# Expert outputs of a routed trunk layer: 29 experts store their slots' products plainly, and each token's row gathers its four

## The chip, the cores and the metric

The kernel runs on one core of one Trainium2 chip. The metric is the device time of one execution in microseconds (us). Before the change, three runs gave 1467.29, 1469.84 and 1470.49 us; the median is 1469.84 us.

## The reference, cut to what matters

512 tokens of width 1024 go through one layer: a mixing sublayer with a LayerNorm, then a routed feed-forward sublayer with a LayerNorm. All data are float32. The change touches only how the outputs of the routed sublayer come together:

```python
top_val, top_idx = lax.top_k(logits, TOP_K)          # 4 of 32 experts for each token
gate = jax.nn.softmax(top_val, axis=-1)
...
gu = xb @ w_gu[e] + b_gu[e]                          # 1024 x 2048 weights for each expert
...
return act @ w_dn[e] + b_dn[e]                       # 1024 x 1024
...
y_sorted = out[dest] * gate.reshape(-1)[order][:, None]
y = jnp.zeros_like(xt).at[tok_sorted].add(y_sorted)  # each token: the sum of its four
...
h = layer_norm(DEEPNORM_ALPHA * h + ffn, ln2_g[l], ln2_b[l])
```

## The kernel before, in words

**Stages.** Up to about 390 us of the profiled span the kernel computes the mixing sublayer, the router and the slots. Each expert has up to 96 slots (`CAP`), a low part of 64 and a high part of 32; the high part is computed only where the expert has more than 64 tokens (`past64`, a branch on a loaded count; always for experts 0 and 31). In this execution 14 of the experts 0 to 30 ran their high part, 13 of them below expert 29; of experts 6 to 26 it is 10. Then `experts` (from line 1365) runs over the 32 experts, and from about 1434 us `tail` does the last LayerNorm and the output.

**Weights.** Each expert needs 12 chunks of 1 MB: eight row blocks of `w_gate_up` and four of `w_down`. All are loaded on SP's queue (line 1193) into a ring of SBUF slots, 18 at the start, whose order is the table `RING`. A load waits until PE has read what stood in its slot, and on the landing of an earlier load: the queue's instructions take their landing counters `DMAHW0` to `DMAHW7` in turn, all DMAs that SP and ACT issue share these eight, and a DMA is issued only when the one before it on its counter has landed. So at most eight are under way.

**Order of one expert.** With k from 0 to 7, `gu_low` multiplies the tokens of the expert by a chunk (line 1285), and `gu_high` those of slots 64 to 95 (line 1290). At k = 3, `load_gu(e + 1)`, `load_dn(e)` and the gather of the tokens of expert e + 2 (`expert_gather`, line 1217, POOL, an indirect DMA of 96 rows of 4 KB) are put in, and the transposes of expert e + 1. Then comes `swiglu`, and then `dn` of the expert before: PE runs gu(e), then dn(e - 1). The tile framework keeps each engine's instructions in the order in which the code gives them.

**Outputs.** `dn` multiplies by `w_down` into PSUM, low part as 128 partitions x 512 (two halves of the columns x 64 slots), high part as 128 x 256 (four quarters x 32 slots). Its inner `out` scales by the gate on ACT into the tile `eo` (line 1335), and an indirect DMA on POOL (line 1336) adds these 128 rows into the DRAM tensor `yd`, at the rows of their tokens. There are 45 such adds, 31 low (experts 0 to 30) and 14 high. `yd` is cleared by three DMAs of `routing_setup` (line 1162) at the start of the program, from a zero tile, on SP. Expert 31 is not added: its products stay on chip and PE sends them to the tokens by 0/1 matrices in `tail`.

**End.** `tail_rows` (line 1529) adds `yd` into the residual `res` by four DMAs of 512 KB on POOL that add to SBUF what they load. `tail` then adds expert 31 and normalizes.

One other place is used below, the loads of the down biases in `bias_loads`, on SP, into 96 partitions x 512 of which the source repeats 32 rows three times:

```python
nc.sync.dma_start(self.braw[q], bass.AP(tensor=b.tensor, offset=b.offset + 512 * q, ap=[[0, 3], [D, NE], [1, 512]]))   # L988
```

Of the kernel before, what the change touches and what calls it, by code (L numbers as in the profile page):

```python
# [24 lines left out]
F32 = mybir.dt.float32  # L25
F32R = mybir.dt.float32r
BF = mybir.dt.bfloat16
I32 = mybir.dt.int32
U32 = mybir.dt.uint32
AF = mybir.ActivationFunctionType  # L30
OP = mybir.AluOpType
# [6 lines left out]
KAPPA = math.exp(-0.5)  # L38
ALPHA = 2.0 ** 0.25
CAP = 96  # L40
OB = 104
PADROWS = 128

# [83 lines left out]
class Trunk:  # L127
# [4 lines left out]
    def setup(self):  # L132
        nc, tc, a = self.nc, self.tc, self.a
        self.cp = cp = self.ctx.enter_context(tc.tile_pool(name="const", bufs=1))
        self.dp = self.ctx.enter_context(tc.tile_pool(name="dram", bufs=1, space=DRAM))
        self.ident = cp.tile([128, 128], F32, name="ident")
        nc.gpsimd.dma_start(self.ident, a["consts"][:, 0:128])
        self.C = cp.tile([128, CONSTS.shape[1] - 128], F32, name="cst")
        self.c = {k: self.C[:, o - 128:o - 128 + n] for k, (o, n) in CAT.items() if k != "ident"}
        e = cp.tile([128, 2], F32, name="eps")  # L140
        self.eps = {v: e[:, q:q + 1] for q, v in enumerate((1e-5, 64e-5))}
        for v, col in self.eps.items():
            nc.vector.memset(col, v)
        self.wd = self.dp.tile([6, T], F32, name="wd")
        self.tab = self.dp.tile([NE * 512, 2], F32, name="tab")
        self.hd = self.dp.tile([T + PADROWS, D], F32, name="hd")
        self.yd, self.yo = (self.dp.tile([T + PADROWS, D], F32, name=n) for n in ("yd", "yo"))

    def params(self):
        nc, a, cp = self.nc, self.a, self.sp  # L150
# [952 lines left out]
    def route_slots(self):  # L1103
# [16 lines left out]
        nc.vector.tensor_tensor(V0, oh, wide(self.val, NE), OP.mult)  # L1120
        nc.vector.tensor_tensor(self.S, c["iota96"].unsqueeze(1).to_broadcast([128, 16, CAP]), wide(dest, CAP), OP.is_equal)

    def route_table(self):
        nc = self.nc
        V = self.V.rearrange("p i k e -> p (i k) e")
        p = self.tbank()
        for k in range(16):
            nc.tensor.matmul(p[0:CAP, 0:64], self.S[:, k], V[:, k], start=(k == 0), stop=(k == 15))
        nc.vector.tensor_scalar(self.tt[:, 0:32], p[0:CAP, 0:32], self.c["pad"][0:CAP], None, OP.add)
        nc.vector.tensor_copy(self.tt[:, 32:64], p[0:CAP, 32:64])  # L1130
# [19 lines left out]
    def routing_setup(self):  # L1150
        nc, sp, c = self.nc, self.sp, self.c
        self.onesb = self.cp.tile([128, 128], BF, name="onesb")
        nc.gpsimd.memset(self.onesb, 1.0)
        self.trib = self.cp.tile([128, 128], BF, name="trib")
        nc.vector.tensor_copy(self.trib, c["mask2"][:, 0:128])
        self.mkb = self.cp.tile([128, NT, NE], BF, name="mkb")
        self.sel0 = self.expert_sel(0)
        self.ro = self.cp.tile([128, 3, NT, 4], F32, name="ro")
        z = self.Sb[0].rearrange("p j v -> p (j v)")
        for c0, n in ((0, 384), (384, 384), (768, 256)):  # L1160
            nc.sync.dma_start(self.hd[T:T + PADROWS, c0:c0 + n], z[:, :n])
            nc.sync.dma_start(self.yd[:, c0:c0 + n].rearrange("(i p) c -> p i c", p=128), z[:, :n].unsqueeze(1).to_broadcast([128, NT + 1, n]))


# [151 lines left out]
    def dn(self, e, aT, wd, n):  # L1316
        nc, mm = self.nc, self.nc.tensor.matmul
        p0 = self.mps.tile([128, 512], F32, name="dn0")
        if e == 0:
            self.dn2 = self.mps.tile([128, 512], F32, name="dn2")[:, 0:256]  # L1320
        p2 = self.dn2

        def high():
            for k in range(NK):
                for c in range(4):
                    mm(p2[32 * c:32 * c + 32], aT[:, 4 + k % 2, 32 * (k // 2):32 * (k // 2) + 32], wd[k][:, 256 * c:256 * c + 256],  # L1326
                       start=(k == 0), stop=(k == NK - 1), skip_group_check=True)

        for k in range(NK):
            for h in range(2):  # L1330
                mm(p0[64 * h:64 * h + 64], aT[:, k % 4, 64 * (k // 4):64 * (k // 4) + 64], wd[k][:, 512 * h:512 * h + 512], start=(k == 0), stop=(k == NK - 1))  # L1331
        def out(g, p):
            w = 512 >> g
            o = self.mw.tile([128, w], F32, name=f"eo{g}")
            nc.scalar.activation(o, p, AF.Copy, scale=self.gate[:, g, e:e + 1])  # L1335
            return nc.gpsimd.indirect_dma_start(out=self.yd.rearrange("t (c f) -> (t c) f", f=w),  # L1336
                                                out_offset=bass.IndirectOffsetOnAxis(ap=self.sidx[:, g, e:e + 1], axis=0),
                                                in_=o, in_offset=None, compute_op=OP.add)

        if e < NE - 1:  # L1340
            first = out(0, p0)

        def past():
            high()
            if e < NE - 1:
                second = out(1, p2)
                self.tc.declare_no_dep(second.ins, first.ins, reason="rows of other slots")
                if self.added is not None:
                    self.after(second, self.added, mybir.DependencyClass.Sync)

        self.past64(n, past)
        if e < NE - 1:
            self.added = first
        if e == NE - 1:
            his = []
            for g, p in enumerate((p0, p2)):
                hi, lo = self.slast[2 * g:2 * g + 2]
                his.append(nc.scalar.activation(hi, p, AF.Copy, scale=self.gate[:, g, e:e + 1]))
                nc.vector.scalar_tensor_tensor(lo, p, self.gate[:, g, e:e + 1], hi, OP.mult, OP.subtract)
            self.warm = self.mw.tile([128, 1], F32, name="warm")  # L1360
            w = nc.scalar.activation(self.warm, self.eps[1e-5], AF.Sqrt)
            for h in his:
                self.after(w, h)

    def experts(self):
        self.xg = [self.mw.tile([128, D], F32, name=f"xg{q}") for q in range(2)]
        xs, xT = {}, {0: self.first_xT()}
        wg, pend, self.added = self.load_gu(0), None, None
        self.route_slots()
        for e in range(NE):  # L1370
            w = wg
            t, sel = xT.pop(e)
            n = self.fill(e)
            p = self.gu(t, sel)
            for k in range(NK):
                self.gu_low(p, k, t, w[k])
                if e == 0:
                    self.gu_high(p, k, t, w[k])
                elif k % 4 == 3:
                    self.past64(n, lambda: [self.gu_high(p, z, t, w[z]) for z in range(k - 3, k + 1)])  # L1380
                if e == 0:
                    if k == 0:
                        self.route_counts()
                        self.route_table()
                        self.tables()
                        xs[1] = self.expert_gather(1)
                    elif k < 5:
                        self.out_init(k - 1)
                if k == 3:
                    if e + 1 < NE:  # L1390
                        wg = self.load_gu(e + 1)
                    wd = self.load_dn(e)
                    if e + 2 < NE:
                        xs[e + 2] = self.expert_gather(e + 2)
                if k == (6 if e == 0 else 3) and e + 1 < NE:
                    xT[e + 1] = self.expert_xT(e + 1, xs.pop(e + 1))
            a = self.swiglu(p)
            if e == NE - 1:
                self.most = self.nc.values_load(self.mxi[0:1, 0:1], min_val=0, max_val=T)
                self.tail_setup()  # L1400
                aT = self.swiglu_T(a)
            if pend:
                self.dn(*pend)
            if e == NE - 1:
                self.tail_rows()
            pend = (e, aT if e == NE - 1 else self.swiglu_T(a), wd, n)
        self.dn(*pend)
# [99 lines left out]
    def tail_setup(self):  # L1507
# [14 lines left out]
        for q, p in enumerate(self.P):  # L1522
            g = q > 1
            m = c["par"][:, q:q + 1] if not g else c["quad"][:, q - 2:q - 1]
            nc.vector.tensor_scalar(p, iota, tk[:, g:g + 1], m, OP.is_equal, OP.mult)

    def tail_rows(self):
        for i in range(NT):
            self.nc.gpsimd.dma_start(self.res[i], self.yd[i * 128:i * 128 + 128], accum_op=OP.add)  # L1529

    def tail(self, out):
# [5 lines left out]
        for i in range(NT):  # L1537
            t = slice(128 * i, 128 * i + 128)
            ps.append([self.tbank() if n == "tr" else self.mps.tile([128, 512], F32, name=n) for n in (("gu0", "gu1"), ("gu2", "tr"), ("tr", "tr"), ("dn0", "dn2"))[i]])
            for q in range(2):  # L1540
# [5 lines left out]
                for x in range(2):  # L1546
                    for z in range(2):
                        mm(p[:, 256 * x:256 * x + 256], self.P[2 + 2 * q + x][:, t], self.slast[2 + z], start=False, stop=x == z == 1)  # L1548
        s = [self.chunk()[0] for _ in range(2)]
        xs = [s[i // 2][:, 1024 * (i % 2):1024 * (i % 2) + 1024] for i in range(NT)]  # L1550
        self.stores = [[] for _ in range(NT)]


# [137 lines left out]
```

## Time and profile before

| what | us |
|---|---|
| runs, lowest / median / highest | 1467.29 / 1469.84 / 1470.49 |
| the profiled execution | 1465.28 |
| its span in the trace | 1463.5 |
| PE busy (matmuls) | 1334.6 (91%) |
| DVE busy | 448.4 (31%) |
| ACT busy | 289.5 (20%) |
| POOL busy | 206.8 (14%) |
| bytes moved, mean rate | 461.88 MB, 316 GB/s |
| the 45 adds of line 1336, issue to landing, min/median/max | 5.8/9.5/11.3 |

The profiled execution is 4.56 us below the median of the runs; 1.8 us of it lie outside the span. Times in the rows below are in us from the start of the span. [...] A DMA share is the mean busy share of the core's 16 DMA engines in the stretch.

### The profile page before, as it was taken

To read this page: it belongs to the slowest core of one execution; us is meant where nothing else is said; L and a number is where in the kernel's file an instruction comes from. 1 tells how busy PE (TensorE), PEld (TensorE's weight loads), DVE (VectorE), ACT (ScalarE), POOL (GpSimd) and SP (SyncE) were. 2 spreads that over 40 slices of the span, in tenths; PEclk is the share of its full clock that TensorE was granted. 3 is DMA by queue.
4 is the path that set the end of the run, shared out by engine and by line. 5 is a ranking of instruction groups with operands and counts; after the bars stand their busy time and mean duration, and the time that the engine had idled before them with its cause. 6 is when DMAs were issued, how large, how long until landed. Compare 5 with 4: busy or idle time off the path is not lost. (4 is left out here: it accounts for less than half of the span.)

```text
span 1463.5 us, 19946 instructions
## 1 busy us (share of the span) xinstructions
PE 1334.6 (91%) x7860; PEld 623.9 (43%) x7861; DVE 448.4 (31%) x1070; ACT 289.5 (20%) x617; POOL 206.8 (14%) x190
## 2 busy tenths in 40 slices
PE   7899978998999999987899999999879878899995
PEld 5677878876533333322233333333323222333323
DVE  5767687788521112111111121111111111211114
ACT  4444342453011111110001111111100100111103
POOL 1211236241001100110001111011100100010100
PEclk9999996899999999999999999999999999999998
DMA  7222233346899999999999999999999999999974
GB/s 253 73 58 72 52 79 99 132 141 269 297 364 375 396 385 403 396 390 395 403 403 397 396 398 399 406 394 394 391 389 402 394 404 395 400 395 415 408 297 118
DMA packets 95232, 461.88 MB, mean 316 GB/s; under 512 B 18084, under 2 KB 26692, under 8 KB 45962
## 3 DMA queue, kind: packets, MB, share of 16 engines
q1 hardware_dynamic: 79962, 435.61, 75.9%
q0 software_dynamic: 10592, 20.49, 6.5%
q10 hardware_dynamic: 4560, 4.15, 0.9%
q8 instruction: 82, 1.34, 0.4%
q14 instruction: 36, 0.29, 0.1%
HBM read 445.97 MB, written 18.10 MB: 317 GB/s over the span
## 5 line engine op out<-in xcount | busy, mean ns | idle before, releaser
L1285 PE MATMUL gu<-wc,xT 128*64 128x512 f32 x2048 | 486.5, 603 | 65.1 <-DMA wc<-w_gate_up 62.2
L1285 PEld LDWEIGHTS gu<-wc,xT 128*64 128x64 f32 x2048 | 143.1, 137 | 388.5 <-issue 243.1
L1298 DVE TENSOR_SCALAR glu<-gu 128x256 f32<-128x256 f32 (+1 forms) x64 | 35.6, 556 | 829.1 <-PE gu L1290 376.6
L1331 PE MATMUL dn<-wc,aT 128*64 128x512 f32 x1024 | 247.5, 603 | 4.2 <-PEq L1278 2.4
L1299 ACT ACTIVATE glu<-glu 128x256 f32<-128x256 f32 (+1 forms) x64 | 33.5, 524 | 543.1 <-DVE glu L1298 543.1
L1217 POOL DMA_INDIRECT xg<-hd,gidx x31 | 30.9, 998 | 670.8 <-PE tr L1230 660.8
L1331 PEld LDWEIGHTS dn<-wc,aT 128*64 128x64 f32 x1024 | 65.1, 136 | 118.9 <-issue 102.3
L1290 PE MATMUL gu<-wc,xT 128*32 128x512 f32 x960 | 111.5, 596 | 0.0
L1336 POOL DMA_INDIRECT yd<-eo,sidx x45 | 70.1, 1557 | 275.2 <-ACT eo L1335 275.2
L222 PE MATMUL pi<-xhi,whi 128*128 128x512 f32 x152 | 65.0, 428 | 15.9 <-ACT whi L172 8.9
L1231 ACT ACTIVATE xT<-tr 128x384 f32<-128x384 f32 x62 | 29.8, 490 | 181.1 <-PE tr L1230 181.1
L223 PE MATMUL pi<-xlo,whi 128*128 128x512 f32 x152 | 63.7, 419 | 0.5 <-DVE xlo L173 0.5
L224 PE MATMUL pi<-xhi,wlo 128*128 128x512 f32 x152 | 62.8, 413 | 0.0
L1290 PEld LDWEIGHTS gu<-wc,xT 128*32 128x32 f32 x960 | 27.0, 109 | 80.1 <-issue 79.8
L1335 ACT ACTIVATE eo<-dn,gate 128x512 f32<-128x512 f32 (+1 forms) x45 | 27.9, 621 | 163.0 <-PE dn L1331 88.9
L1326 PE MATMUL dn<-wc,aT 128*32 128x256 f32 x960 | 56.1, 381 | 1.0 <-ACT aT L1313 1.0
L173 POOL TENSOR_TENSOR wlo<-wraw,whi 128x512 fp32r<-128x512 f32 (+1 forms) x28 | 39.0, 1397 | 124.3 <-ACT whi L172 120.3
L1326 PEld LDWEIGHTS dn<-wc,aT 128*32 128x32 f32 x960 | 29.5, 110 | 34.0 <-issue 14.6
L172 ACT ACTIVATE whi<-wraw 128x512 fp32r<-128x512 f32 (+1 forms) x54 | 33.8, 634 | 47.8 <-DMA wraw<-w_in 21.9
L222 PEld LDWEIGHTS pi<-xhi,whi 128*128 128x128 f32 x152 | 30.0, 197 | 26.2 <-ACT whi L172 8.5
L1301 DVE SCALAR_TENSOR_TENSOR glu<-glu 128x256 f32<-128x256 f32 (+1 forms) x64 | 35.4, 555 | 7.2 <-ACT glu L1299 6.2
L1312 PEld LDWEIGHTS tr<-ident,glu 128*128 128x128 f32 x192 | 25.5, 208 | 26.4 <-DVE sel L1237 19.5
(489 smaller groups left out, 1501.1 us busy)
## 6 DMA issues: line engine op xcount, KB each, us to landing
wc<-w_gate_up SPq DMA_DIRECT2D x256, 1024.0 KB
wc<-w_down SPq DMA_DIRECT2D x128, 1024.0 KB
wraw<-w_in SPq DMA_DIRECT2D x46, 256.0 KB
wraw<-w_out SPq DMA_DIRECT2D x16, 256.0 KB
xraw<-xT SPq DMA_DIRECT2D x4, 512.0 KB
res<-x SPq DMA_DIRECT2D x4, 512.0 KB
hd<-res ACTq DMA_DIRECT2D x4, 512.0 KB
res<-yd POOLq DMA_DIRECT2D x4, 512.0 KB
```

The costliest lines, as they stand in the source:

```text
L172: self.hi_ins = nc.scalar.activation(hi, src, AF.Copy)
L173: return (eng or nc.vector).tensor_tensor(lo, src, hi, OP.subtract)
L222: nc.tensor.matmul(p, hi, xh, start=(k == 0), stop=False)
L223: nc.tensor.matmul(p, hi, xl, start=False, stop=False)
L224: nc.tensor.matmul(p, lo, xh, start=False, stop=(k == NK - 1))
L1285: mm(p[q][64 * h:64 * h + 64], xT[:, k, 0:64], w[:, 1024 * q + 512 * h:1024 * q + 512 * h + 512], start=False, stop=(k == NK - 1))
L1290: self.nc.tensor.matmul(p[2][32 * c:32 * c + 32], xT[:, k, 64:96], w4[:, c], start=False, stop=(k == NK - 1), skip_group_check=True)
L1298: nc.vector.tensor_scalar(out[:, c], g, 7.0, None, OP.min)
L1301: nc.vector.scalar_tensor_tensor(out[:, c], ln[:, c], 1.0, out[:, c], OP.add, OP.mult)
L1326: mm(p2[32 * c:32 * c + 32], aT[:, 4 + k % 2, 32 * (k // 2):32 * (k // 2) + 32], wd[k][:, 256 * c:256 * c + 256], start=(k == 0), stop=(k ...
L1331: mm(p0[64 * h:64 * h + 64], aT[:, k % 4, 64 * (k // 4):64 * (k // 4) + 64], wd[k][:, 512 * h:512 * h + 512], start=(k == 0), stop=(k == N ...
L1336: return nc.gpsimd.indirect_dma_start(out=self.yd.rearrange("t (c f) -> (t c) f", f=w), out_offset=bass.IndirectOffsetOnAxis(ap=self.sidx[ ...
```

## The change

For experts 0 to 28 the products are no longer added by token but stored by slot, into a new DRAM tensor `ed` of 29 x 96 rows and one row of zeros. A low part is stored by a DMA that ACT issues, a high part by one that POOL issues. `routing_setup` also clears the slots 64 to 95 of all 29 experts in `ed` and the last row, by six DMAs more on SP. `route_rows` computes, for each token and each of its four experts, the row of `ed` (the zero row for experts 29, 30, 31 and dropped tokens). Near the end, 16 indirect DMAs on POOL (`rows_get`) fetch 128 rows of 4 KB each, one for each block of 128 tokens and each of the four choices, and 16 adds on DVE (`rows_add`) put them into `res`. Experts 29 and 30 are added into `yd` as before, and expert 31 is sent by PE as before. The gathers go into the two `xg` tiles and into two chunks of the ring (`gx`), which `tail` took later before and now takes over; so the loads behind them use slots two places further on.

```diff
+ADDED = 29
...
+        self.ed = self.dp.tile([ADDED * CAP + 1, D], F32, name="ed")
...
+    def route_rows(self):
+        nc, cp = self.nc, self.cp
+        v = cp.tile([128, 2, NT, 4], F32, name="erow")
+        self.eidx = cp.tile([128, NT, 4], I32, name="eidx")
+        u, m = v[:, 0], v[:, 1]
+        nc.vector.tensor_scalar(u, self.ro[:, 0], float(CAP), -float(ADDED * CAP), OP.mult, OP.add)
...
+        nc.vector.tensor_scalar(self.eidx, u, float(ADDED * CAP), None, OP.add)
...
             nc.sync.dma_start(self.hd[T:T + PADROWS, c0:c0 + n], z[:, :n])
+            nc.sync.dma_start(self.ed[ADDED * CAP:ADDED * CAP + 1, c0:c0 + n], z[0:1, :n])
+            nc.sync.dma_start(self.ed[0:ADDED * CAP, c0:c0 + n].rearrange("(e s) c -> s e c", s=CAP)[64:CAP],
+                              z[0:CAP - 64, :n].unsqueeze(1).to_broadcast([CAP - 64, ADDED, n]))
...
             nc.scalar.activation(o, p, AF.Copy, scale=self.gate[:, g, e:e + 1])
+            if e < ADDED:
+                n = w >> 3
+                r = CAP * e + 64 * g
+                return (nc.gpsimd if g else nc.scalar).dma_start(self.ed[r:r + n].rearrange("s (c f) -> c s f", f=w), o)
             return nc.gpsimd.indirect_dma_start(out=self.yd.rearrange("t (c f) -> (t c) f", f=w),
...
-        if e < NE - 1:
+        if ADDED <= e < NE - 1:
             self.added = first
...
+                    if e + 2 == NE:
+                        self.rows_get(0, 2, self.xg)
+                if e == 4 and k == 0:
+                    self.route_rows()
+                if e == NE - 1 and k == 3:
+                    self.rows_add(0, 2)
+                    self.rows_get(6, 2, self.xg)
...
                 aT = self.swiglu_T(a)
+                self.rows_add(2, 4)
+                self.rows_get(8, 4, self.gx)
+                self.rows_add(6, 2)
+                self.rows_get(12, 2, self.xg)
+                self.rows_add(8, 4)
+                self.rows_get(14, 2, self.gx[:2])
+                self.rows_add(12, 4)
...
+            if e + 2 == NE:
+                s = [self.chunk()[0] for _ in range(2)]
+                self.gx = [s[i // 2][:, 1024 * (i % 2):1024 * (i % 2) + 1024] for i in range(NT)]
+                self.rows_get(2, 4, self.gx)
...
+    def rows_get(self, n0, m, dst):
+        for q in range(m):
+            n = n0 + q
+            self.got[n] = dst[q]
+            self.nc.gpsimd.indirect_dma_start(out=dst[q], out_offset=None, in_=self.ed,
+                                              in_offset=bass.IndirectOffsetOnAxis(ap=self.eidx[:, n // 4, n % 4:n % 4 + 1], axis=0))
+    def rows_add(self, n0, m):
+        for n in range(n0, n0 + m):
+            r = self.res[n // 4]
+            self.nc.vector.tensor_tensor(r, r, self.got.pop(n), OP.add)
...
-        s = [self.chunk()[0] for _ in range(2)]
-        xs = [s[i // 2][:, 1024 * (i % 2):1024 * (i % 2) + 1024] for i in range(NT)]
+        xs = self.gx
```

The rows of code in the built programs show three places. First ACT, at the end of the `dn` of one expert with the high part in its branch; `eo` is the scaled product, `tr` and `aT` belong to the next expert, and the numbers at a DMA are the dimensions of its DRAM side. Before:

```order
L1335 ACTIVATE eo_8464<-dn_3835,gate 128x256
L1278 UNCONDITIONAL_BRANCH x2
L1335 ACTIVATE eo_8428<-dn_8411,gate 128x512
L1313 ACTIVATE aT<-tr 128x512
L1313 ACTIVATE aT<-tr 128x256
L1270 TENSOR_LOAD cnti
```

With the change, the same place:

```order
L1353 ACTIVATE eo_8479<-dn_3842,gate 128x256
L1296 UNCONDITIONAL_BRANCH x2
L1353 ACTIVATE eo_8443<-dn_8426,gate 128x512
L1331 ACTIVATE aT<-tr 128x512
L1357 DMA ed<-eo_8443 2x64x512
L1331 ACTIVATE aT<-tr 128x256
```

The low store stands on ACT between two copies; its DRAM side has an outermost dimension of 2 (two halves of the columns), then 64 slots and 512 columns.

Second SP, the weight loads in the middle of the experts with what each waits for (`PE` is the slot's last reader). Before:

```order
L1193 DMA wc<-w_down 128x2048 [waits DMAHW4_49,PE_49]
L1193 DMA wc<-w_gate_up 128x2048 [waits DMAHW5_49,PE_49]
L1278 UNCONDITIONAL_BRANCH
L1193 DMA wc<-w_gate_up 128x2048 [waits DMAHW6_49,PE_49]
L1193 DMA wc<-w_gate_up 128x2048 [waits DMAHW7_49,PE_49]
L1193 DMA wc<-w_gate_up 128x2048 [waits DMAHW0_49,PE_49]
L1193 DMA wc<-w_gate_up 128x2048 [waits DMAHW1_49,PE_49]
```

With the change:

```order
L1211 DMA wc<-w_gate_up 128x2048 [waits DMAHW0_49,PE_49]
L1211 DMA wc<-w_gate_up 128x2048 [waits DMAHW2_49,PE_49]
L1211 DMA wc<-w_gate_up 128x2048 [waits DMAHW3_49,PE_49]
L1211 DMA wc<-w_gate_up 128x2048 [waits DMAHW4_49,PE_49]
L1296 UNCONDITIONAL_BRANCH
L1211 DMA wc<-w_gate_up 128x2048 [waits DMAHW5_49,PE_49]
L1211 DMA wc<-w_gate_up 128x2048 [waits DMAHW6_49,PE_49]
L1211 DMA wc<-w_gate_up 128x2048 [waits DMAHW7_49]
L1211 DMA wc<-w_down 128x2048 [waits DMAHW0_49]
L1296 UNCONDITIONAL_BRANCH
L1211 DMA wc<-w_down 128x2048 [waits DMAHW1_49,PE_49]
```

Once for each expert the loads leave one counter out (here `DMAHW1`): ACT's store has it. Seven loads stand between, and the next load on that counter waits until the store has landed.

Third POOL, the end of the program. Before:

```order
L1511 IOTA wc 128x512
L1278 COMPARE_AND_BRANCH
L1336 DMA yd<-eo_9854,sidx 2560x256
L1278 UNCONDITIONAL_BRANCH
L1278 ISA
L1278 UNCONDITIONAL_BRANCH
L1336 DMA yd<-eo_9818,sidx 1280x512
L1529 DMA res_2732<-yd 128x1024 x2
L1529 DMA res_2735<-yd 128x1024 x2
```

With the change:

```order
L1573 DMA wc<-ed,eidx 128x1024 x4
L1573 DMA xg_3397<-ed,eidx 128x1024
L1573 DMA xg_3398<-ed,eidx 128x1024
...
L1358 DMA yd<-eo_9636,sidx 1280x512
L1552 IOTA wc 128x512
L1573 DMA wc<-ed,eidx 128x1024 x6
L1296 COMPARE_AND_BRANCH
...
L1358 DMA yd<-eo_9867,sidx 1280x512
L1583 DMA res_2739<-yd 128x1024 x2
L1583 DMA res_2742<-yd 128x1024 x2
```

The gathers stand on POOL ahead of the last adds into `yd` and of the four loads of `tail_rows`. Four more gathers, not shown, stand just ahead of this piece.

## Rows read from the trace of the kernel before

**Rows 1.** The page: DMA share and rate, 40 slices of 36.6 us
```profile
DMA  7222233346899999999999999999999999999974
GB/s 253 73 58 72 52 79 99 132 141 269 297 364 375 396 385 403 396 390 395 403 403 397 396 398 399 406 394 394 391 389 402 394 404 395 400 395 415 408 297 118
```

**Rows 2.** Waits of PE, stretch 390 to 1374: us in total, times, longest
```profile
PE gu L1285 <- DMA wc<-w_gate_up: 62.2, 74, 2.9
```

**Rows 3.** Waits of SP's queue, stretch 390 to 1463, same columns
```profile
SPq L1193 <- DMA wc<-w_gate_up: 536.1, 214, 4.4
SPq L1193 <- DMA wc<-w_down: 227.2, 105, 4.9
SPq L1193 <- PE gu L1285: 52.8, 27, 10.3
```

**Rows 4.** Busy time by stretch, low add of expert 6 to that of 27
```profile
core 0: us, PE busy (x) PEld busy (x) DVE busy (x) ACT busy (x) POOL busy (x), PEclk, DMA share, GB/s
620.00:1326.00 706.00, 641.13 (x3678) 216.85 (x3676) 89.92 (x210) 78.02 (x159) 68.46 (x52) 1.00 1.02 397
```

**Rows 5.** Timeline of POOL: start, duration, piece, the idle time before it
```profile
620.15 1.57 POOL L1336 DMA_INDIRECT yd<-eo,sidx  x1 [3.76 <-ACT eo L1335]
...
1049.69 1.01 POOL L1217 DMA_INDIRECT xg<-hd,gidx  x1 [23.35 <-PE tr L1230]
1055.74 1.56 POOL L1336 DMA_INDIRECT yd<-eo,sidx  x1 [5.04 <-ACT eo L1335]
1057.80 1.55 POOL L1336 DMA_INDIRECT yd<-eo,sidx  x1 [0.50 <-ACT eo L1335]
...
1325.86 1.54 POOL L1336 DMA_INDIRECT yd<-eo,sidx  x1 [32.05 <-ACT eo L1335]
```

**Rows 6.** Stretches without an add (two), and with the adds of expert 28
```profile
1358.00:1360.00 2.00, 2.00 (x18) 0.66 (x12) 0.00 (x0) 0.47 (x1) 0.87 (x1) 1.00 1.02 426
1384.00:1386.00 2.00, 2.00 (x44) 1.23 (x40) 0.00 (x0) 0.00 (x0) 0.00 (x0) 1.00 1.05 426
1364.00:1370.00 6.00, 5.84 (x28) 2.11 (x26) 0.00 (x0) 0.00 (x0) 0.00 (x0) 1.00 1.07 352
```

**Rows 7.** Stretch in which the accumulating loads of `tail_rows` run alone
```profile
1432.00:1440.00 8.00, 5.92 (x46) 3.91 (x42) 5.17 (x14) 4.42 (x9) 1.07 (x2) 1.00 1.07 210
```

**Rows 8.** Line 988 on SP's queue, and the stretch while one load moves
```profile
L988 SPq DMA_DIRECT2D wraw<-b_down x2: 728/791/854, 302.9 to 308.2; - x2
306.00:308.00 2.00, 2.00 (x10) 1.65 (x9) 2.00 (x7) 1.14 (x3) 1.08 (x1) 1.00 0.19 72
```

**Rows 9.** Stretch after the gather at 1049.69, with both adds of expert 19
```profile
1054.00:1068.00 14.00, 11.55 (x66) 3.35 (x56) 0.00 (x0) 1.92 (x4) 3.10 (x2) 1.00 1.04 359
```

**Rows 10.** Front: two stretches, and ACT's wait for w_in, 0 to 60
```profile
20.00:24.00 4.00, 4.00 (x20) 2.96 (x18) 1.38 (x2) 1.84 (x3) 0.00 (x0) 1.00 1.04 362
28.00:40.00 12.00, 12.00 (x52) 9.35 (x51) 6.24 (x11) 6.48 (x10) 0.00 (x0) 1.00 0.59 187
ACT whi L172 <- DMA wraw<-w_in: 11.8, 8, 4.0
```

**Rows 11.** Waits of PE, stretch 1374 to 1434
```profile
PE gu L1285 <- DMA wc<-w_gate_up: 0.7, 1, 0.7
```

**Rows 12.** Stretches after the last weight load was issued at 1405
```profile
1416.00:1418.00 2.00, 2.00 (x12) 0.71 (x10) 0.71 (x2) 0.00 (x0) 0.00 (x0) 1.00 0.46 182
1422.00:1424.00 2.00, 2.00 (x10) 0.48 (x8) 0.00 (x0) 0.38 (x1) 1.34 (x1) 1.00 0.12 51
```

**Rows 13.** The chain that ended last: start, us, piece
```profile
1422.66 5.85 DMA yd<-eo,sidx
1430.96 9.83 DMA res<-yd
```

More of the change, by code (lines that the diff above doesn't have):

```diff
@@ L1121, in route_slots @@
         nc.vector.tensor_tensor(self.S, c["iota96"].unsqueeze(1).to_broadcast([128, 16, CAP]), wide(dest, CAP), OP.is_equal)
+    def route_rows(self):
[4 more added lines that the diff above has]
+        nc.vector.tensor_scalar(u, self.ro[:, 0], float(CAP), -float(ADDED * CAP), OP.mult, OP.add)
+        nc.vector.tensor_tensor(u, u, self.ro[:, 2], OP.add)
+        nc.vector.tensor_scalar(m, self.ro[:, 2], float(CAP), None, OP.is_lt)
+        nc.vector.scalar_tensor_tensor(m, self.ro[:, 0], float(ADDED), m, OP.is_lt, OP.mult)
+        nc.vector.tensor_tensor(u, u, m, OP.mult)
+        nc.vector.tensor_scalar(self.eidx, u, float(ADDED * CAP), None, OP.add)
     def route_table(self):
@@ L1367, in experts @@
         xs, xT = {}, {0: self.first_xT()}
+        self.got = {}
         wg, pend, self.added = self.load_gu(0), None, None
```

## The prediction

> **What bounds the kernel now.** I read the 40 slices first: from the tenth of them to the thirty-eighth the DMA engines are 9 or more tenths busy and move 364 to 415 GB/s [rows 1]. Then the waits: PE waits in 390:1374 almost only for weights, 62.2 us in 74 pieces [rows 2]. SP's queue waits for the landing of earlier loads, 536.1 + 227.2 us, and only 52.8 us for PE to free a slot [rows 3]. So the expert phase runs at the pace of the loads. From the low add of expert 6 at 620.15 to that of 27 at 1325.86 are 705.71 us, 33.6 for each of 21 experts [rows 5]. In this stretch PE is busy 641.13 us, 30.5 for an expert, at a DMA share of 1.02 [rows 4]: PE has 3.1 us to spare for each expert, the DMA engines nothing.
>
> What do the 33.6 us hold? Undisturbed, the loads move 426 GB/s [rows 6], 26.6 for each of 16 engines, so a chunk of 1.049 MB takes 2.46 us and the 12 of an expert 29.5. While both adds of expert 28 land, 6 us move 352 x 6 = 2.112 MB [rows 6]; less the adds' 0.393 MB, the weights got 1.719, worth 4.03 us, and the adds cost 1.97. By the accumulating loads alone, 210 GB/s [rows 7], they would cost 0.393/210 = 1.87. I take 1.9: 1.27 for a low add (0.262 MB), 0.63 for a high one. After the gather, 14 us hold 359 x 14 = 5.026 MB [rows 9]; less two adds and the gather (96 x 4 KB = 0.393 MB) 4.240 are weights, 9.95 us; 14 - 9.95 - 1.9 leaves 2.15 for the gather and what else came. Sum, with 10 high adds on 21 experts: 29.5 + 1.27 + 0.30 + 2.15 = 33.2, against 33.6 measured. The bound is accounted for.
>
> **Removed.** 29 low and 13 high adds: 29 x 1.27 + 13 x 0.63 = 45.0 us of all DMA engines, on the path since nothing else sets the pace there.
>
> **Low stores: the term that decides.** Each has 0.262 MB. The nearest price that looks kind is the plain rate, 0.262/426 = 0.62 us, 18.0 for 29. But the store's DRAM side is split as 2 x 64 x 512. The trace has one pair of DMAs with such a small outermost dimension, the bias loads of line 988, 3 x 32 x 512 on one side and 96 partitions on the other, rows of 2 KB like the store's. While one moves, nothing else does, and the DMA share is 0.19 at 72 GB/s [rows 8]: 3/16 is 0.1875, so 3 engines worked at 24 GB/s each, and 13 stood idle. A store with an outermost 2 should then run on 2 engines, 0.131 MB each, 0.131/24 = 5.46 us of each of the two. Nothing in the instruction differs from expert to expert, so I take the same two each time. They have 29.5 us of weights for each expert like the others, and a chunk is complete only with its last engine: the two set the pace for all. 29 x 5.46 = +158.4 us. The ends are 18.0 and 158.4, and I take the latter, because its row has the same shape, row length and kind of queue; that it is a load and not a store is what keeps the other end alive.
>
> [...]
>
> **High stores.** 4 x 32 x 256 from POOL: by the same reading 4 engines, 0.033/24 = 1.37 us each. If the four change from store to store, a quarter falls on the two: 13 x 1.37/4 = 4.4; if they are always the same, 17.8. I take 4.4. On POOL and ACT themselves a store replaces or adds one DMA issue, hidden: ACT is busy 78.02 of 706 us, POOL 68.46 [rows 4]. The copy of `aT` behind the store on ACT is read only by the next `dn`.
>
> **The wait that is added.** A store takes one of the eight landing counters, and a load stands behind it on that counter. Seven loads are between, 7 x 2.46 = 17.2, with the store 22.7 us of the two engines' work. Served first, the store lands in 5.5 us and holds nobody; alternating with weight rows of 8 KB, its 64 rows let 64 x 8 KB = 0.524 MB of an engine's weights pass, 19.7 us, and it lands after 25.2: 2.5 us without a new load. So 0 to 2.5 for an expert, 0 to 72 in all. I take 0.7, 20 us: the adds got 1.9 of 6 us in rows 6, neither served first nor last, and a late load hurts only once the queue has run dry.
>
> **Gathers.** 16 of 128 x 4 KB = 0.524 MB. Twelve can be issued before the weights have all landed. By bytes 0.524/426 = 1.23 each; by the gather above with all that came beside it, 2.15 x 128/96 = 2.87. I take 1.6, nearer to the bytes because the 2.15 holds other things: 12 x 1.6 = +19, bounds 15 to 34. The additions on DVE (16 of 128x1024) lie beside PE work: DVE is busy 13% of the stretch [rows 4]. `route_rows`, six small DVE instructions, is hidden the same way; should that cover be gone, a microsecond or two.
>
> **Front.** Clearing 29 x 32 rows of 4 KB moves 3.80 MB; at the 362 GB/s of such a stretch [rows 10] 10.5 us. In 28:40 the engines are idle 0.41 x 12 = 4.9 us [rows 10], so up to 5.6 us could delay `w_in`, for which ACT waits already, 11.8 us in all [rows 10]. Bounds 0 and 6; I take 2, nearer to 0 because in 28:40 PE is busy throughout [rows 10], so that loads a little late cost it nothing yet. The six more issues on SP are in that.
>
> **End.** Before, the chain ends in the last add, 5.85 us, then the loads of `tail_rows`, 9.83 us [rows 13]. Now the last gathers stand ahead of both on POOL: 0 to 8 us later. Against that, in 1374:1434 PE waits 0.7 us for weights [rows 11], it runs behind them; slower loads let it catch up, worth up to 6. And the engines do not end together: at 1422:1424 a share of 0.12 is left, about two engines, where it was 0.46 six us earlier [rows 12]. If the laggards are not the two with the stores, these have up to 10 us to give, once. Together -16 to +8; I take -4.
>
> **Sum.** -45.0 + 158.4 + 4.4 + 20 + 19 + 2 - 4 = +154.8. The profiled execution took 1465.28, so 1620.1; it stood 4.56 below the median of 1469.84, so the median should come to 1624.6, and I say 1625. Per expert that is 33.6 - 1.27 - 0.3 + 5.46 + 0.16 + 0.7 = 38.4 us before the gathers.
>
> **Rivals.**
> *All 16 engines, gathers in the way.* If a store, unlike a load, spreads: -45.0 + 18.0 + 13 x 0.31 = -23.0, +19 gathers, +2 front, +6 end: +4, about 1474. For it: rows 8 show a load. Against: the same pattern fields decide there.
> *Faster: all 16 engines, gathers hidden.* PE waits only 0.7 us for weights after 1374 [rows 11]. If the saving puts the loads at least 19 us ahead of PE by the first gather (eight loads in flight are 19.7), twelve gathers cost nothing: -23.0 + 2 + 6 = -15, about 1455. It decides at that 19: below it each microsecond is paid. Against it, again rows 8.
> *Two engines, but others each time.* Then each engine has one eighth of the stores, the load is even, -23 as above, and what remains is the hold, 29 x about 1, with 19 + 2 + 4: about +31, 1500. For it: no row shows which engines serve.
> *The hold in full.* 72 instead of 20: +207, about 1677.
>
> **How the numbers follow.** Two engines always the same, with a hold of up to about 2 us: 0.82. The hold in full: 0.05. Other engines each time: 0.03. Sixteen engines at +4: 0.05; sixteen and faster: 0.05. The main case's own bounds: at the low end stores at 26.6 GB/s (-15), gathers by bytes (-4), no hold (-20), end -16 (-12): 1574; at the high end hold 2 (+38), end +8 (+12): 1675. All at one end together is unlikely, so I give 1575 to 1675, with 0.8 inside; the rest is left out below and above. A measurement of this kernel can tell 0.2%, 2.9 us, from no change. Faster by more: 0.05, the third rival. Within: 0.02, a part of the +4 case. Slower: 0.93.
>
> **What would show it.** Right: low stores of some 128 packets of 2 KB whose landing takes 15 to 30 us under load; spacing of the experts near 38 us; a DMA share well under 1 in the 100-us stretches (29.5/38.4 and the smaller things: about 0.85 to 0.92) and some 350 GB/s instead of 397; PE's waits for weights up from 62 us to about 200. Wrong: a share that stays at 1.02 and stores landing within 6 us would mean 16 engines. If the spacing is 33 and the end late, the gathers were the matter. The prediction fails altogether if the stores' engines are not fixed.

## The result and the profile after

The changed kernel takes 1674.28 us (median of 4 runs, 1673.1 to 1674.6) against 1468.57 for the kernel before on the same chip: ratio 1.1401, 95% interval 1.1379 to 1.1422. It is slower by 206 us, 49 more than the 1625 forecast, at the very top of the range of 1575 to 1675. The profiled span is 1672.3 us, 208.8 more than before.

The page's DMA rows of the kernel after, which answer to [rows 1]:

```profile
DMA  6522233458888888888888888887888888888895
GB/s 190 155 76 57 50 90 101 141 179 313 337 317 332 309 347 340 343 347 340 339 346 338 336 347 347 321 320 316 341 350 345 337 338 343 340 359 355 342 381 134
```

The engines are no longer full in the expert phase: 8 tenths, and 309 to 359 GB/s where it was 364 to 415. From 620 us to the last low store the share is 0.85 and the rate 339 GB/s, the answer to the 1.02 and 397 of [rows 4]:

```profile
620.00:1533.00 913.00, 745.14 (x4144) 241.59 (x4143) 99.52 (x234) 89.16 (x175) 29.66 (x33) 0.98 0.85 339
```

What SP's queue waits for there, the answer to [rows 3] (us in total, times, longest):

```profile
SPq L1211 <- DMA ed<-eo: 604.9, 28, 26.3
SPq L1211 <- DMA wc<-w_gate_up: 184.1, 64, 4.9
SPq L1211 <- DMA wc<-w_down: 168.5, 84, 3.6
```

28 loads wait for a low store to land, up to 26.3 us each. Such a wait is not yet a loss: before, this queue waited 763 us for landings [rows 3] with the engines at a share of 1.02 [rows 4]. The loss shows in the DMA share. PE's waits from 390 on, the answer to [rows 2]; the last two are new, and the second was 1.8 us before:

```profile
PE gu L1303 <- DMA wc<-w_gate_up: 130.4, 129, 3.1
PE dn L1349 <- DMA wc<-w_down: 55.4, 33, 4.9
PE gu L1281 <- DVE glu L1318: 18.6, 1, 18.6
PE tr L1330 <- DVE glu L1320: 10.9, 1, 10.9
```

One expert in the middle. ACT's timeline (start, us, piece), where it issues the low store:

```profile
1024.24 0.69 ACT L1353 ACTIVATE eo<-dn,gate 128x512 f32<-128x512 f32 x1 [4.39 <-PE dn L1349]
1024.96 0.99 ACTq L1357 DMA_DIRECT2D ed<-eo  x1
```

The stretches of 2 us some 17 us later (the last three columns are PE's granted clock as a share of its full speed, the DMA share and GB/s):

```profile
1042.00:1044.00 2.00, 0.78 (x6) 0.20 (x4) 0.00 (x0) 0.00 (x0) 0.00 (x0) 1.00 0.99 410
1044.00:1046.00 2.00, 2.00 (x13) 0.45 (x13) 0.00 (x0) 0.00 (x0) 0.00 (x0) 1.00 0.35 137
1046.00:1048.00 2.00, 2.00 (x24) 0.65 (x20) 0.00 (x0) 0.00 (x0) 0.00 (x0) 1.00 0.13 53
1048.00:1050.00 2.00, 2.00 (x16) 0.47 (x10) 0.75 (x2) 0.29 (x1) 0.00 (x0) 1.00 0.12 49
1050.00:1052.00 2.00, 2.00 (x10) 0.79 (x6) 1.85 (x5) 0.76 (x2) 0.00 (x0) 1.00 0.53 66
1052.00:1054.00 2.00, 2.00 (x9) 0.51 (x9) 1.60 (x5) 0.00 (x0) 0.00 (x0) 1.00 0.78 328
```

In the 19 us of 1025:1044 all engines are full, a share of 1.01. Then 14 engines have done all that was issued, and a share of 0.13 and 0.12, 2 of 16, goes on alone at 49 to 53 GB/s. What these two move can be read from the DMA queues in 1046:1049 (q1 carries SP's loads, q10 ACT's store; packets, MB, share of 16 engines):

```profile
q1 hardware_dynamic: 17, 0.12, 9.7%
q10 hardware_dynamic: 17, 0.03, 3.0%
```

Here one row of the store (2 KB) moves for each row of weights (8 KB), the alternation from which the prediction took its landing of 25.2 us. So the two still have weights to move as well, and most of the 49 to 53 GB/s is weights. About 25 us after its issue the store lands, and for a microsecond no engine moves anything:

```profile
1050.00:1051.00 1.00, 1.00 (x7) 0.17 (x3) 0.85 (x3) 0.12 (x1) 0.00 (x0) 1.00 0.00 0
```

Then the held load moves, and two more microseconds pass before the engines are full again. In the packets of the trace each low store of the experts 6 to 28 ends so, with all 16 engines empty for 0.79 to 1.42 us.

To see where the 209 us lie, I cut each profiled run at ACT's scaled low products (the 31 `eo` of 128x512 in ACT's timeline): the first, that of expert 6, that of expert 28, and the end of the span.

| kernel | first `eo` | expert 0 to 6 | one expert, 6 to 28 | 28 to end | median us |
|---|---|---|---|---|---|
| before | 441.2 | 178.0 | 33.68 | 103.3 | 1469 |
| after | 468.0 | 206.7 | 38.99 | 139.8 | 1674 |
| act_split | 463.5 | 187.1 | 32.95 | 129.5 | 1508 |
| pool_same | 468.1 | 178.8 | 33.16 | 132.2 | 1510 |
| act_perm_2 | 468.2 | 202.4 | 39.05 | 136.9 | 1670 |
| act_perm_4 | 464.2 | 191.0 | 34.71 | 131.4 | 1553 |
| zero_only | 464.9 | 177.2 | 33.70 | 102.8 | 1489 |
| act_split_nogather | 467.5 | 186.6 | 32.99 | 100.8 | 1484 |
| split_late | 450.5 | 185.8 | 32.98 | 127.0 | 1497 |
| split_late_order | 455.6 | 187.0 | 32.95 | 122.5 | 1492 |
| split_late_order2 | 456.6 | 186.4 | 33.00 | 126.4 | 1496 |

After less before: front +26.8, experts 0 to 28 +28.7 + 22 x 5.31 = +145.5, end +36.5. The rows are those of the profiled execution; for split_late that is one of 1490.71 us, 6.4 below its median, and for the kernel before one of 1465.28; the others lie within 2 us of theirs.

### The profile page after: what moved, and what is told of

Read it like the earlier page. It is cut to its first block, busy times and chain, and to the rows that moved or that the text cites. A ratio compares the mean times of both kernels' runs of the same rounds, so it can differ in the third digit from the quotient of the medians.

```text
span 1672.3 us, 19961 instructions
## 1 busy us (share of the span) xinstructions
PE 1378.1 (82%) x7860; PEld 624.8 (37%) x7861; DVE 465.8 (28%) x1092; ACT 292.7 (18%) x617; POOL 168.0 (10%) x177
## 5 line engine op out<-in xcount | busy, mean ns | idle before, releaser
L1303 PE MATMUL gu<-wc,xT 128*64 128x512 f32 x2048 | 494.4, 604 | 132.1 <-DMA wc<-w_gate_up 130.4
L1349 PE MATMUL dn<-wc,aT 128*64 128x512 f32 x1024 | 268.0, 645 | 57.4 <-DMA wc<-w_down 55.4
L1303 PEld LDWEIGHTS gu<-wc,xT 128*64 128x64 f32 x2048 | 134.2, 137 | 474.4 <-DMA wc<-w_gate_up 256.9
L1349 PEld LDWEIGHTS dn<-wc,aT 128*64 128x64 f32 x1024 | 69.3, 144 | 184.1 <-issue 109.8
L1235 POOL DMA_INDIRECT xg<-hd,gidx x31 | 30.2, 975 | 932.7 <-PE tr L1248 922.6
L1281 PE MATMUL gu<-mb,sel 128*128 128x512 f32 x64 | 28.6, 450 | 18.6 <-DVE glu L1318 18.6
L174 ACT ACTIVATE whi<-wraw 128x512 fp32r<-128x512 f32 (+1 forms) x54 | 33.4, 634 | 55.5 <-DMA wraw<-w_in 33.2
L1330 PE MATMUL tr<-ident,glu 128*128 128x128 f32 x192 | 32.1, 303 | 10.9 <-DVE glu L1320 10.9
```

Of the source, the lines that this page charges most:

```text
L174: self.hi_ins = nc.scalar.activation(hi, src, AF.Copy)
L1303: mm(p[q][64 * h:64 * h + 64], xT[:, k, 0:64], w[:, 1024 * q + 512 * h:1024 * q + 512 * h + 512], start=False, stop=(k == NK - 1))
L1330: nc.tensor.transpose(p[:, z * 128:z * 128 + 128], t2[:, (z0 + z) // 2, z % 2], self.ident)
```

## The experiments

**How many engines a store gets.** `act_split` sends each half of the columns by itself:

```diff
-                return (nc.gpsimd if g else nc.scalar).dma_start(self.ed[r:r + n].rearrange("s (c f) -> c s f", f=w), o)
+                if g:
+                    return nc.gpsimd.dma_start(self.ed[r:r + n].rearrange("s (c f) -> c s f", f=w), o)
+                for c in range(2):
+                    d = nc.scalar.dma_start(self.ed[r:r + n, w * c:w * c + w], o[n * c:n * c + n])
+                return d
```

> The low store of an expert goes out as two DMAs from ACT, one for each half of the columns, 64 x 512 on both sides, in place of one 2 x 64 x 512; bytes, rows of 2 KB and queue stay. My theory (two engines carry each low store, and the load behind it on its landing counter is held): a low store costs 0.62 us of all engines, lands within some 10 us and holds nobody, so about +4 us against the kernel before, 1473, between 1460 and 1490, at an expert spacing near 33.6 us and a DMA share near 1.0. Rival (stores of 2 KB rows are dear or the counter is dear whatever the engines): stays above 1600.

Measured 1508.33, ratio 1.0282 (1.0243 to 1.0321): 166 us of the loss are gone. From expert 6 on one expert takes 32.95 us, 0.73 less than before, close to the 0.8 (23 us over 29 experts) that spread stores promised. But 1508 lies outside the range that I gave: 42 us remain against the kernel before where I expected 4. By the table they are 22 in the front, 9 in the experts 0 to 6 and 26 at the end, less 16 for the 22 experts from 6 to 28. Nor do these stores hold nobody. SP's queue still waits for them (from 390 us on), although the engines are full, as in 1100:1200:

```profile
SPq L1211 <- DMA ed<-eo: 281.1, 55, 22.1
1100.00:1200.00 100.00, 90.69 (x486) 30.79 (x484) 12.93 (x30) 11.57 (x23) 3.67 (x4) 0.98 1.01 404
```

At this share of 1.01 no cost of a held load shows, as the loads ahead of it keep the engines busy.

`act_perm_2` and `act_perm_4` keep the two DMAs, their bytes and rows, and give each an outermost dimension of 2 or of 4:

```diff
-                    d = nc.scalar.dma_start(self.ed[r:r + n, w * c:w * c + w], o[n * c:n * c + n])
+                    d = nc.scalar.dma_start(self.ed[r:r + n, w * c:w * c + w].rearrange("(b a) f -> a b f", a=2), o[n * c:n * c + n])
```

> As act_split, but each half is written as 2 x 32 x 512 with the slots' rows in another order (even rows, then odd ones), so that the outermost dimension is 2 again; the rows that the gathers fetch are then those of other slots. Two engines theory: 1674, between 1640 and 1700, and a DMA share that falls to about 0.13 at some time for each expert. Rival (what helped act_split is that there are two smaller DMAs): near act_split.

> As act_perm_2 with an outermost dimension of 4 (4 x 16 x 512; slots' rows in another order). Four engines with 0.066 MB each, 2.73 us for an expert: 2.73 - 1.57 = +1.2 us an expert over the kernel before, 34 in all; the store lands after about 12.6 us, before the load behind it is due, so no hold; with gathers and front about +57: 1525, between 1505 and 1550. Rival: as act_perm_2, either 1674 or near act_split.

Measured 1669.60, ratio 1.1377 (1.1322 to 1.1433), and 1552.99, ratio 1.0583 (1.0531 to 1.0634). With the same two DMAs, bytes and rows, an outermost dimension of 2, 4 and 64 gives 39.05, 34.71 and 32.95 us for an expert, and one DMA with a 2 gives what two with a 2 give (38.99). So in these runs the outermost dimension decides, and the number of DMAs does not. By the prediction's terms two engines need 33.68 - 1.27 - 0.29 + 5.46 + 0.16 = 37.7 us, and 39.0 were measured: 1.3 are left for the hold, about the time for which all engines stand empty after each store (0.79 to 1.42 in the kernel after). Four engines need 35.0 by the same sum, against 34.71, but that does not show that nothing is held there. SP's queue waits for these stores too, and when the second store of an expert lands, some 16 us after its issue at 865.95, the share sinks:

```profile
SPq L1211 <- DMA ed<-eo: 461.0, 57, 19.6
882.00:884.00 2.00, 2.00 (x24) 0.53 (x18) 0.00 (x0) 0.00 (x0) 0.00 (x0) 1.00 0.43 125
```

So the sum comes out, but the runs do not separate its terms. The total of act_perm_4 came out 28 above my 1525, mostly by the front and the end that act_split has too.

act_perm_2 also speaks for it that two stores of ACT in a row take the same engines. ACT issues both within 1.52 us, yet in 1023:1037 exactly the 64 rows of one of them move, and those of the other follow in 1037:1047 (the 68 packets there are 64 rows and four of 4 bytes, two at 1037 and two at 1046). I infer the same engines from this order; that two stores on different engines would move side by side, no run shows.

```profile
1021.79 1.52 ACTq L1360 DMA_DIRECT2D ed<-eo  x2
q10 hardware_dynamic: 64, 0.13, 2.4%
q10 hardware_dynamic: 68, 0.13, 3.4%
```

**Whether the engines change, and the counters.** `pool_same` leaves the pattern 2 x 64 x 512 and only moves the issue:

```diff
-                return (nc.gpsimd if g else nc.scalar).dma_start(
+                return nc.gpsimd.dma_start(
```

> The low store keeps its pattern 2 x 64 x 512 but POOL issues it, as the high ones, so it takes none of the eight counters that the loads use. My theory has two parts, 4.1 us an expert for the two engines and 3 for the hold. If POOL's DMAs also use the same two engines each time, only the hold goes: 1674 - 29 x 3 = about 1590. [...]

Measured 1509.89, ratio 1.0287 (1.0249 to 1.0326): 80 below the 1590, although the front takes 26.9 us more than before and the end 28.9, about as much as in act_split. One expert takes 33.16 us. SP's queue again waits for no store:

```profile
SPq L1211 <- DMA wc<-w_gate_up: 534.5, 217, 5.2
SPq L1211 <- DMA wc<-w_down: 231.5, 107, 3.4
SPq L1211 <- PE gu L1303: 52.5, 30, 10.3
```

The stores are narrow still: POOL's 29 of 256 KB land 19.0 us after their issue (median), where act_split's 58 of 128 KB take 7.2:

```profile
ed<-eo POOLq DMA_DIRECT2D x29, 256.0 KB, 19.0
ed<-eo ACTq DMA_DIRECT2D x58, 128.0 KB, 7.2
```

So narrow stores from POOL cost nearly nothing, 33.16 us for an expert beside act_split's 32.95. Had they always sat on the same two engines, these would by the sum above still need 37.7, hold or no hold. I infer that the load is even over the engines, that is, that POOL's 29 stores here change their engines; which engines serve a store is seen in no run.

Whether the store of the next expert from ACT takes the same two again, no run shows, and in the spacing of the kernel after it could not show. Each hold there ends with all engines empty, and from an empty start any two would take as long. So the 39.0 does not rest on "the same two each time", and pool_same, which takes away the counter and, by that inference, changes the engines as well, does not say what either alone would give.

The counters alone can be seen in the early experts, where PE lags behind the loads and stores are issued late. Experts 0 to 6 take 187.1 us in act_split, whose stores are spread but take two counters each, and 178.8 in pool_same, which takes none: 8 us that I put down to the counters. In that time SP's queue waits for act_split's stores 67.1 us in all, once 22.1 us, though they land within some 9 us of their issue: here a load was held by a store that was not issued yet. No run isolates the 8 us. The wait and the stretch 500:600 of act_split, then that stretch of pool_same:

```profile
SPq L1211 <- DMA ed<-eo: 67.1, 9, 22.1
500.00:600.00 100.00, 93.39 (x469) 34.31 (x469) 13.75 (x32) 12.67 (x26) 4.63 (x5) 1.00 0.90 349
```

```profile
500.00:600.00 100.00, 98.18 (x496) 37.69 (x493) 13.67 (x32) 13.33 (x27) 8.17 (x9) 1.00 1.02 398
```

**The front.** `zero_only` is the kernel before with `ed` and its clearing.

```diff
+            nc.sync.dma_start(self.ed[ADDED * CAP:ADDED * CAP + 1, c0:c0 + n], z[0:1, :n])
+            nc.sync.dma_start(self.ed[0:ADDED * CAP, c0:c0 + n].rearrange("(e s) c -> s e c", s=CAP)[64:CAP],
+                              z[0:CAP - 64, :n].unsqueeze(1).to_broadcast([CAP - 64, ADDED, n]))
```

> The kernel before with the clearing of ed alone (six more DMAs on SP at the start; nothing reads ed). With the change the first scaled product on ACT came at 468.0 us where it was 441.2, 26.8 later, with the split stores 463.5, 22.3 later. Theory: this clearing delays the loads of w_in, and all that follows: +22 to +27 us, 1488 to 1494. Rival (my prediction): the delay is hidden, +2, 1468. Rival: the loads of the weights run ahead meanwhile and some of it is won back: about +10.

Measured 1488.75, ratio 1.0152 (1.0123 to 1.0181): +20 to +23 us (span 1486.4, 22.9 more), as the theory said, and none of it won back. Its stretches of 4 us:

```profile
28.00:32.00 4.00, 2.40 (x11) 1.60 (x9) 1.19 (x3) 1.85 (x3) 0.00 (x0) 1.00 0.92 324
32.00:36.00 4.00, 1.92 (x4) 0.80 (x4) 1.29 (x2) 3.64 (x5) 0.00 (x0) 0.84 0.08 29
36.00:40.00 4.00, 0.43 (x2) 0.00 (x0) 3.86 (x3) 0.00 (x0) 0.00 (x0) 0.50 0.00 0
40.00:44.00 4.00, 2.55 (x6) 2.09 (x7) 3.90 (x8) 0.00 (x0) 0.00 (x0) 0.50 0.37 109
```

SP's queue in the same time (start, us, piece), and where ACT and DVE split the pair of loads issued at 22.31 into its two terms:

```profile
22.31 2.67 SPq L203 DMA_DIRECT2D wraw<-w_in  x2
25.04 2.16 SPq L1167 DMA_DIRECT2D yd<-M  x1
41.42 0.93 SPq L203 DMA_DIRECT2D wraw<-w_in  x2
34.54 1.14 ACT L174 ACTIVATE whi<-wraw 128x512 fp32r<-128x512 f32 x2
40.71 1.29 DVE L175 TENSOR_TENSOR wlo<-wraw,whi 128x512 fp32r<-128x512 f32 x2
```

PE, busy throughout before [rows 10], now does 0.43 us in 36:40, at a granted clock of 0.50. The engines are nearly full until 32 (0.92 in 28:32), and the rows of the two loads of `w_in` issued at 22.31 end at about 30.2, where they ended at 26.2 before: 4 us late. ACT and DVE split them, and only then is there a buffer for the next pair, which SP issues at 41.42 (29.32 before). The DMA engines idle meanwhile (0.00 in 36:40). The lateness grows on that way because the built order has changed too: ACT takes the work of line 588, which before came behind this split and those of two later pairs, ahead of it, and splits at 34.54 instead of 26.82. So the engines' order is not simply that of the code, as I had written above: an added DMA moved it. How much of the 12 us is the landing and how much the order, no run separates. This comes three times, once for each piece of the clearing: by the start of the same matmuls PE is 11, then 20, then 24 us behind the kernel before. `split_late` takes the clearing of the slots out of the front:

```diff
+                        if i == 0:
+                            z = t.nc.gpsimd.dma_start(t.ed[0:ADDED * CAP].rearrange("(e s) c -> s e c", s=CAP)[64:CAP],
+                                                      t.yd[0:CAP - 64].unsqueeze(1).to_broadcast([CAP - 64, ADDED, D]))
+                            t.after(z, t.exp_ins, mybir.DependencyClass.Sync)
```

> act_split with the slots 64 to 95 of ed cleared later: one DMA on POOL, at about 240 us, that copies rows of zeros from yd, 3.8 MB, in place of three on SP at the start. Theory (the clearing at the start costs 22 us, and at 240 us the DMA engines have room, 0.2 to 0.4 busy): 1508 - 22 = 1486, between 1482 and 1492. Rival: the bytes cost 10 us wherever they are moved: about 1496.

Measured 1497.11, ratio 1.021 (1.018 to 1.0241), 11 less than act_split: the rival's number, but not its reason. The first `eo` comes at 450.5, still 9.3 late. Yet up to 290 us nothing is late: the same matmuls start 1 us earlier than before at 100 us and 8.6 earlier at 293, so the loss that zero_only shows went with the clearing. The copy, issued at 260.5, fills the engines (share 1.00 in 260:270), but the delay comes after it, between 295 and 320 us, when PE waits for `w_out`. Again the order has changed. Behind the copy POOL now does line 444 and waits for it, and splits the next `w_out` only at 300.81 (267.83 before):

```profile
293.14 1.86 POOL L444 TENSOR_TENSOR mlc<-mlc,so 128x384 f32<-128x384 f32 x2 [31.69 <-DVE mlc L443]
300.81 3.12 POOL L175 TENSOR_TENSOR wo<-wraw,wo 128x512 fp32r<-128x512 f32 x2
PE ps L868 <- POOL wo L175: 6.8, 1, 6.8
```

That the order and not the bytes cost these 18 us is read from the rows; no run isolates it.

**The end.** `act_split_nogather` leaves out `rows_get`'s DMAs and `rows_add`'s additions, and with them the sums of experts 0 to 28:

```diff
-            self.nc.gpsimd.indirect_dma_start(out=dst[q], out_offset=None, in_=self.ed,
...
-            self.nc.vector.tensor_tensor(r, r, self.got.pop(n), OP.add)
+            self.got.pop(n)
```

> act_split without the 16 gathers and the 16 additions on DVE (the sums of experts 0 to 28 are left out of the output). In act_split PE waited 12.0 + 10.4 us for swiglu on DVE at the end, and the low store of expert 28 to the end took about 129 us where the kernel before took 102. Theory (the gathers and the additions that stand ahead of swiglu on DVE cost the end): 26 us less than act_split, about 1482. Rival (gathers cost only their bytes, 12 x 1.6 = 19, or nothing): 1489 to 1508.

Measured 1483.82, ratio 1.0117 (1.0088 to 1.0146). From expert 28 to the end it takes 100.8 us, with them 129.5: 28.7 for 16 gathers and additions. The theory's number came, but the run takes away the gathers' bytes together with the additions, so it cannot tell the theory from its rival. In the kernel after one sees a mechanism at work. DVE's timeline:

```profile
1566.37 1.22 DVE L1579 TENSOR_TENSOR res<-res,xg 128x1024 f32<-128x1024 f32 x1 [45.87 <-DMA xg<-ed,eidx]
1570.17 1.22 DVE L1579 TENSOR_TENSOR res<-res,xg 128x1024 f32<-128x1024 f32 x1 [2.58 <-DMA xg<-ed,eidx]
1571.31 0.42 DVE L1316 TENSOR_SCALAR glu<-gu 128x256 f32<-128x256 f32 x1
```

PE's timeline at the same time:

```profile
1572.21 0.77 PE L1281 MATMUL gu<-mb,sel 128*128 128x512 f32 x1 [18.55 <-DVE glu L1318]
```

The swiglu of expert 30 stands on DVE behind two additions that wait for their gathers, and PE stands still for it. `split_late_order` orders the additions behind swiglu:

```diff
+            for x in self.sw:
+                self.after(d, x)
```

> split_late with the additions on DVE put behind swiglu: rows 0 and 1 are added after the swiglu of expert 30, all others after that of expert 31. Theory (PE waits 12.0 + 10.4 us because swiglu stands behind additions that wait for their gathers): PE's two waits go, 22 us, but the last gathers and additions then end later, 5 to 15 us: 1470, between 1463 and 1480. Rival (the gathers' bytes, not the order, make the end late): no gain over split_late.

Measured 1492.07, ratio 1.0163 (1.013 to 1.0197), outside my range. PE's two waits for swiglu are gone, and yet the end takes 122.5 us where split_late took 127.0: 4.5 of 21.6 us. I had named the buffers as what was late next, and tried it: `split_late_order2` lets rows 0 to 7 be added before the last swiglu.

```diff
-            for x in self.sw:
+            for x in self.sws[NE - 2 if n < 8 else NE - 1]:
                 self.after(d, x)
```

> split_late_order, but rows 0 to 7 may be added once the swiglu of expert 30 is done, and only rows 8 to 15 wait for that of expert 31. In split_late_order the rows 2 to 5 had landed some 12 us before the swiglu of expert 31 and held their buffers, and the gathers behind them on POOL, the last add into yd and the loads of tail_rows came late. Theory (the buffers and POOL's order now end the chain): the last gathers come about 10 us sooner, 1482, between 1476 and 1488. Rival (the gathers' transfers, or the additions on DVE, end it): no gain, 1490 to 1494.

Measured 1495.97, ratio 1.0202 (1.0172 to 1.0231): no gain, and 126.4 us at the end. PE waited again for the last swiglu (10.4 us), because the order that the framework made of it put an addition in its middle, so this run tests the buffers only in part. What is left is the transfers. The stretch 1440:1450, first of act_split_nogather, then of split_late_order:

```profile
1440.00:1450.00 10.00, 9.09 (x72) 2.83 (x72) 0.00 (x0) 1.43 (x3) 3.42 (x5) 1.00 0.70 227
```

```profile
1440.00:1450.00 10.00, 8.76 (x73) 2.81 (x69) 4.91 (x5) 1.89 (x3) 3.68 (x3) 1.00 1.02 410
```

With the gathers the engines are still full 72 to 82 us after the product of expert 28 (1367.5), where without them the share is down to 0.70 at 60 to 70 us (1379.9). 16 gathers by bytes are 16 x 1.23 = 19.7 us; split_late_order's end less that without gathers is 21.7. That the bytes explain nearly all of it is worked out, not isolated by a run.

No version tried beats the kernel before. The reason can be summed from the table. Spread stores save 16 us in the experts 6 to 28, the experts 0 to 6 lose 9 of these again, and the end with its 16 gathers on full engines takes 19 to 26 more. What is left of the front (14.4 us in split_late_order) comes on top.

## Why the prediction was right, and where it was not

- **Bound.** Right: the expert phase followed the loads. Two readings were off and decide nothing. The engines are 9 tenths busy from the twelfth slice on, not the tenth [rows 1]. And the gather in [rows 9] moved 60 rows of 4 KB, 0.25 MB, not 96, since it leaves out slots without a token; by the same sum it cost 1.8 us, not 2.15.
- **Low stores, +158.4.** Right in that two engines carry each store (by the share of 0.12 to 0.13) and in size: the forecast spacing was 38.4 us, measured 38.99; with removed adds, high stores and hold I had 137.8 for 29 experts, and 145.5 were measured. "The same two each time" is shown by no run, and it was not needed. As each hold empties all engines, another two each time would by this reasoning have cost about the same here, so my rival of +31 was priced too low, and my choice between +31 and +154.8 rested on a question that the kernel after does not decide.
- **The hold, 20 us.** Right in mechanism, a little small: 39.0 - 37.7 = 1.3 us for an expert, some 35 us, between the 0.7 taken and the bound of 2.5. The row by row alternation, which I took as that bound, is what the queues show (17 and 17 rows in 1046:1049). The full-hold rival gave 1677, close to 1674, but not for its reason.
- **The front, +2.** This step failed: 26.8 in the profile of after, 22.9 by zero_only alone, far over the bound of 6. I counted the bytes against the idle share and reasoned that busy PE has loads in hand. It has one pair: `w_in` goes through two buffers in turn, and a late pair delays the next (in zero_only 4 us late, and the next issued at 41.42 instead of 29.32). I looked at the rate, not at the chain load, split, free buffer, load, nor at the order on ACT and DVE, which the new DMAs changed.
- **Gathers and end, +19 - 4.** Too small by 22. The gathers' 19 for twelve of them stands beside 21.7 for all sixteen. Missed were the order on DVE, which I called work beside PE while swiglu waited behind it (127.0 - 122.5 = 4.5 of the end), and that the gathers must wait for the slow last store: the first gather starts 24 us after its issue at 1533.2 in the kernel after, 10 in act_split, more than the 10 by which their ends differ. The -4 for PE catching up is not seen.
- **Sum.** 154.8 predicted, 208.8 in the profiles: 25 missing in the front, 22 at the end, 8 in the stream. That 1674 still lies in the range is in part luck: its upper end of 1675 was made of a hold of 2 us and an end 12 later than taken, and has nothing in it for the front.

## What to carry to other kernels

Read the DRAM side of each DMA in a full stream by its outermost dimension: 2 in front of 64 x 512 cost 166 us here when ACT issued it, with the same bytes and rows, and two DMAs of 64 x 512 instead of one removed it. Look also for stores that share landing counters with a prefetch stream: here loads waited up to 26.3 us for a store to land, and in the early experts of act_split up to 22.1 us for stores that land within some 9 of their issue. The wait showed in the time where the engines ran dry, 38.99 us for an expert at a share of 0.85, and not in act_split's later experts, 32.95 at 1.01. And before 3.8 MB are called hidden in idle time, look for a chain of two buffers beside them, and before additions are called beside the matmuls, for what stands behind them on their engine. Last, a DMA added or moved changed the built order of other engines in zero_only and split_late, so such a run tests more than its bytes: compare the order before the time.

## What the runs showed of the hardware that was not expected

- With the same narrow store one expert takes 39.0 us when ACT issues it and 33.2 when POOL does.
- In the kernel after, store and load rows alternate one for one on the two engines that they share: 17 and 17 packets in 1046:1049. The store's 17 rows of 2 KB, 0.0348 MB, took 3.0% of 16 engines' 3 us, 24 GB/s for an engine, as the bias loads of [rows 8], though they write DRAM.
- In zero_only PE's granted clock fell to 0.50 in 36:40, after it had been busy 1.92 us of the four before, and it was still 0.50 in 40:44: the first matmuls after the wait took 2.55/6 = 0.43 us each, where 20 took 4.00 in [rows 10].
